# A hybrid attention block in f32: k and v of one half of the second branch by seven products, with the weight sums made in DRAM

## The chip, the core and the metric

The kernel runs on one core of a Trainium2 chip. A core has five engines with queues of their own: TensorE (PE) for matmuls, with its weight load listed apart as PEld, VectorE (DVE), ScalarE (ACT), GpSimd (POOL) and SyncE (SP). Transfers are issued from the queues of SP, ACT and POOL. The metric is the device time of one execution in microseconds, the median over runs. A profiled execution gives a span, from the first to the last recorded instruction, and its own time, which is some 2 us longer.

## The reference

One decoder block over 512 tokens of width 1024. The normalised input is projected, two attention branches of 8 heads of 64 read the projections, each is multiplied by a SiLU gate, projected back, and both are merged by sigmoid gates.

```python
h = rms_norm(x, norm_g[layer])
proj = h @ w_in[layer]
fq, fk, fv, fz, mq, mk, mv, mz, ga, gb, fl = split_cols(proj, IN_SPLITS)
...
y_fox = from_heads(fox_attention(q, k, v, log_f)) * jax.nn.silu(fz)
q = partial_rope(rms_norm(to_heads(mq, MOBA_HEADS), moba_q_g[layer]), positions)
k = partial_rope(rms_norm(to_heads(mk, MOBA_HEADS), moba_k_g[layer]), positions)
v = to_heads(mv, MOBA_HEADS)
y_moba = from_heads(moba_attention(q, k, v)) * jax.nn.silu(mz)
merged = (jax.nn.sigmoid(ga + b_gate[layer, 0]) * (y_fox @ w_fox[layer])
          + jax.nn.sigmoid(gb + b_gate[layer, 1]) * (y_moba @ w_moba[layer]))
x = x + merged @ w_out[layer]
```

The part that the change touches most is `mk` and `mv` for the first four heads of the second branch: 256 columns of k and 256 of v, each the product of the 512x1024 normalised input with a 1024x256 block of `w_in`. The names of blocks are `f` or `m` for the branch, `q`, `k`, `v` or `z`, and `a` or `b` for the half of the heads: `mka` is k of the first half of the second branch.

## The kernel before

Precision: a float32 operand is split into a high part (rounded to the matmul format, by a ScalarE copy) and a low part (the rest, by a VectorE subtraction), and every product is three matmuls, high by high, high by low and low by high. For weights this is `split` (L138, with L141 and L143); the split input is kept in `Gh` and `Gl`, transposed, eight blocks of 128 rows by 512 tokens.

Weights come in as blocks of 512 KB (512 rows by 256 columns) on SP's queue, into the four buffers of the tag "wr". `stream` puts a load and a preparation for each block into two lists, in the order of the list `order` (L997), and `pump` (L189) works the lists off: it issues a load when the buffer four places before has been prepared, and prepares blocks up to three ahead of the unit of matmuls that is about to run.

A unit of an ordinary projection (`unit`, `unit_mm`, L308) is one tile of 128 tokens: 24 matmuls of 256 columns into one PSUM bank (8 row blocks, three matmuls each). For q and k, `evac_qk` copies the bank out (L322), and after every second tile `norm_qk` (L331) computes the norms, with two operations on POOL (L343, L345), and `do_rope` turns the first 16 columns, on POOL too. For v, `evac_v` splits the bank into high and low parts (L352, L353).

The work runs in stages. The start loads and normalises x and computes the first projections. The stage "attention" holds four attention groups, (f,a), (f,b), (m,a) and (m,b), each mixed by `inter` (L1026) with units of projections as filler: `plan` (L1066) says which. With group (f,b) go `mka`, `mva` and `mza`. A group begins with transposes of q and k (`Tr`, `p_qT` and `p_kT`, L528 and L530), copies of them on SP's and ACT's queues (L541, L549 to L551), and memsets on POOL that `zero_kl` (L452) issues once. Within an engine the framework fixes the order of the instructions when the kernel is built; an engine takes them in that order.

The stage "gates" computes the gate projections `ga` and `gb`, for which the kernel uses a scheme of seven products of half the size in place of eight (`group`, L715). The input is cut into four blocks, A11, A12, A21, A22, by halves of the tokens and halves of the rows of x, and the weights likewise. Sums of the input blocks, S1 to S4, are made once by `make_sums` (L265) during the first attention group, stored to DRAM on ACT's queue (L284), and loaded back by `load_sums` (L287) on POOL's queue when "gates" begins. The sums of the weight blocks are made on VectorE (`sub`, L722) in the "wr" buffers. `PRODUCTS` gives the order of the products and the accumulator of each. The last stage, the output projection, uses seven products too, with two sums by accumulating transfers on POOL's queue (L897).

Of the kernel before, what the change touches and what calls it, by code (L numbers as in the profile page):

```python
# [7 lines left out]
F32 = mybir.dt.float32  # L8
F32R = mybir.dt.float32r
AF = mybir.ActivationFunctionType  # L10
OP = mybir.AluOpType
# [18 lines left out]
def fox_moba_kernel(ctx: ExitStack, tc, xT, x, w_in, w_fl, w_fox, w_moba, w_out, cst, rope, out):  # L30
# [171 lines left out]
    def stream(name):  # L202
        first_prep[name] = len(preps)
        if name[0] == "G":
            group(name)
            return
# [54 lines left out]
    S_dram = [dr.tile([4, P, 4, HT], F32, name=f"s_dram{hl}") for hl in "hl"]  # L261
# [3 lines left out]
    def make_sums(k):  # L265
# [6 lines left out]
        for o, x, y, op in ((s3, a[:, 0:HT], a[:, HT:S], OP.subtract), (s1, a[:, HT:S], b[:, HT:S], OP.add),  # L272
                            (s2, s1, a[:, 0:HT], OP.subtract), (s4, b[:, 0:HT], s2, OP.subtract)):
            V.tensor_tensor(out=o, in0=x, in1=y, op=op)
        for i, f in enumerate((f0, f1)):
            hl = [tl("sh", F32R), tl("sl", F32R)]
            A.activation(hl[0], f, AF.Copy)
            V.tensor_tensor(out=hl[1], in0=f, in1=hl[0].bitcast(F32), op=OP.subtract)
            out.extend((d[2 * i:2 * i + 2, :, k, :].rearrange("s p t -> p s t"),
                        t.bitcast(F32).rearrange("p (s t) -> p s t", t=HT)) for d, t in zip(S_dram, hl))  # L280
# [6 lines left out]
    def load_sums():  # L287
        for i in range(4):
            SB.append([stage["pool"].tile([P, 4, HT], F32R, name=f"S{i}{hl}") for hl in "hl"])
            for d, t in zip(S_dram, SB[i]):  # L290
                nc.gpsimd.dma_start(out=t.bitcast(F32), in_=d[i])

    def left(what, k):
        if what[0] == "S":
            return [x[:, k] for x in SB[S_AT[what]]]
        t, kk = int(what[1]) - 1, 4 * (int(what[2]) - 1) + k
        return [x[:, kk, t * HT:(t + 1) * HT] for x in (Gh, Gl)]
# [85 lines left out]
    def first_qk(name, tags):  # L383
# [10 lines left out]
        return banks  # L394

# [316 lines left out]
    PRODUCTS = (("A11", 1), ("S3", 3), ("A12", 2), ("S2", 1), ("S1", 1), ("A22", 3), ("S4", 1))  # L712
    groups = {}

    def group(name):  # L715
# [6 lines left out]
        def sub(o, a, b):  # L722
            V.tensor_tensor(out=o, in0=a, in1=b, op=OP.subtract)

        def load(key, nm, hf):
            def go():
                R[key] = sb.tile([P, 4, CW], F32, name=f"wr_{nm}{hf}", tag="wr", bufs=WR)
                nc.sync.dma_start(out=R[key], in_=w_in[COLS[nm] // CW, :, 4 * hf:4 * hf + 4, :])
            return go

        def prep(n):

            def go():
                if n == 1:
                    sub(R["11"], R["12"], R["11"])
                    sub(R["12"], R["22"], R["12"])
                elif n == 3:
                    sub(R["12"], R["22"], R["11"])
                elif n == 5:
                    sub(R["21"], R["21"], R["12"])  # L740
                key = ("11", "12", "21", "12", "11", "21", "22")[n]
                B[n] = split(R[key], CW, f"{name}{n}")
            return go
        for key, nm, hf, last in (("11", wa, 0, 4), ("12", wb, 0, 5), ("22", wb, 1, 6), ("21", wa, 1, 5)):
# [29 lines left out]
        def evac(n):  # L774
# [8 lines left out]
            elif n == 1:  # L783
                keep(3, 3)
            elif n == 2:
                add(st["u"][0], 0, 1, 2)
# [10 lines left out]
        def finish(q):  # L797
            u, j0 = st["u"][q], 2 * i + 4 * q
            bg = C_BG + (0 if ga else 8)
            for c in range(2):  # L800
                if q == 0:
                    A.activation(u[:, c, :], u[:, c, :], AF.Sigmoid, bias=col(bg + j0 + c))
                else:
                    A.activation(u[:, c, 0:HT], two(st[1])[:, c, :], AF.Sigmoid, bias=col(bg + j0 + c))
                    A.activation(u[:, c, HT:S], u[:, c, HT:S], AF.Sigmoid, bias=col(bg + j0 + c))
# [191 lines left out]
    order = ["fqa", "fka", "fza", "fzb", "fva", "fqb", "fkb", "fvb", "mqa", "mka", "mva", "mza", "mqb", "mkb", "mvb", "mzb", "wf0", "wf1", "wf2", "wf3",  # L997
# [59 lines left out]
    for k, u in enumerate(fz):  # L1057
        u()
        if k < 3:
# [5 lines left out]
    rope_tables()  # L1065
    plan = (("f", "a", C_FQ, C_FK, ["fqb", "fkb", "fvb", "mqa"]),  # L1066
            ("f", "b", C_FQ, C_FK, ["mka", "mva", "mza"]),
# [4 lines left out]
    for n in range(4):  # L1072
# [24 lines left out]
        inter(body + ([following] if n < 3 else []) + tail, fill)  # L1097
# [131 lines left out]
```

## Time and profile before

| What | Value |
|---|---|
| Median of 3 runs | 425.77 us (425.74 to 426.47) |
| The profiled execution's own time | 425.43 us |
| Its span | 423.4 us |
| Matmuls | 2913 recorded |
| Bytes moved by DMA | 58.21 MB, 137 GB/s in the mean |

The page of the profile lists busy time by engine, then the span in 40 slices with the busy share of each in tenths, then the chain of waits followed back from the last instruction, then the costliest groups of instructions (line, engine, operation, output and inputs, count, busy time, mean in ns, idle time before and what ended it), and last the transfers with the time from issue to landing. Views of the trace give the timeline of one engine, the instructions of one line or one tile, and the busy times of all engines in chosen stretches. A row of a timeline has start, duration, engine, line, operation, output and inputs; a row of stretches has begin and end, length, busy time and count for PE, PEld, DVE, ACT and POOL, the granted clock of TensorE as a share, the share of the DMA engines, and GB/s.

### The profile page before, as it was taken

How to read it: one execution, taken by the hardware profiler on the slowest of the kernel's cores; microseconds unless marked ns; L12 is line 12 of the kernel's file. 1: busy time of each engine (PE TensorE's matmuls, PEld its weight loads, DVE VectorE, ACT ScalarE, POOL GpSimd, SP SyncE). 2: the span in 40 equal slices, each digit the busy share in tenths (PEclk: the TensorE clock that was granted, in tenths of full speed). 3: DMA queues.
4: the chain of work that ended last, by engine and by line, in shares of the span. 5: the costliest groups of instructions: out<-in, count | busy, mean ns of one | idle time of the engine just before them, and what ended most of it. 6: DMA issues, size and time to landing. Idle time of an engine off the chain costs nothing.

```text
span 423.4 us, 7713 instructions
## 1 busy us (share of the span) xinstructions
PE 417.7 (99%) x2913; PEld 388.9 (92%) x2913; DVE 326.8 (77%) x570; ACT 269.5 (64%) x515; POOL 106.3 (25%) x120
## 2 busy tenths in 40 slices
PE   8999999999999999999999999999999999999996
PEld 6998899999999998899998888899999989988885
DVE  4679977899967768578676787767979698689883
ACT  4986327778767767567656686756656535686450
POOL 1065730225136550016660202140000000022330
PEclk9999999999999999999999999999999999999999
DMA  7973334666263323314123222473042603696484
GB/s 242 396 257 112 100 101 127 183 198 211 77 209 108 100 78 125 82 45 124 31 96 114 88 74 82 154 279 110 31 170 66 233 2 121 206 253 116 100 142 157
DMA packets 25621, 58.21 MB, mean 137 GB/s; under 512 B 3064, under 2 KB 7856, under 8 KB 25584
## 3 DMA queue, kind: packets, MB, share of 16 engines
q1 hardware_dynamic: 13392, 38.11, 27.7%
q10 hardware_dynamic: 8800, 11.21, 8.7%
q0 software_dynamic: 3392, 8.39, 8.5%
q8 instruction: 23, 0.38, 0.3%
q14 instruction: 14, 0.11, 0.1%
HBM read 48.11 MB, written 6.32 MB: 129 GB/s over the span
## 4 chain that ended last, share of the span: by engine, by line
PE 97%; DMA 1%; SPq 0%; DVE 0%; issue 0%; ACT 0%
PE pb_GB L762 3%; PE pb_GA L762 3%; PE pb_GB L759 3%; PE pb_GA L759 3%; PE pb_GB L761 3%; PE pb_GA L761 3%; PE po L950 3%; PE po L949 3%; PE po L948 3%; PE lg L565 2%; PE pv L620 2%; PE pv L619 2%; PE lg L564 2%; PE pf L690 2%; PE pf L689 2%; PE pm L690 2%
## 5 line engine op out<-in xcount | busy, mean ns | idle before, releaser
L343 POOL TENSOR_TENSOR ff<-ss,mh 128x8 f32<-128x8 f32 x16 | 32.0, 2005 | 71.0 <-DVE ss L341 63.2
L567 DVE CUSTOM_DVE_ANT_0 p<-lg,mask 128x128 f32<-128x128 f32 (+1 forms) x64 | 30.6, 488 | 15.7 <-PE lg L565 15.3
L569 ACT ACTIVATE p<-p,negm 128x128 f32<-128x128 f32 (+1 forms) x64 | 35.6, 557 | 10.0 <-DVE negm L567 9.7
L897 POOL DMA_DIRECT2D wr_o<-in_w_out_dram x4 | 4.9, 1293 | 95.4 <-DMA wr_o<-in_w_out_dram 87.2
L143 DVE TENSOR_TENSOR wl_GA<-wr_ga,wh_GA 128x1024 fp32r<-128x1024 f32 x14 | 16.9, 1223 | 7.6 <-ACT wh_GA L141 5.8
L141 ACT ACTIVATE wh_GA<-wr_ga 128x1024 fp32r<-128x1024 f32 x14 | 14.6, 1059 | 9.9 <-PE pb_GA L761 4.9
L141 ACT ACTIVATE wh_GB<-wr_gb 128x1024 fp32r<-128x1024 f32 x14 | 14.6, 1059 | 9.5 <-PE pm L689 3.5
L564 PE MATMUL lg<-KH,QS 128*128 128x128 f32 (+1 forms) x64 | 20.3, 327 | 0.0
L910 ACT ACTIVATE wh_o<-wr_o 128x1024 fp32r<-128x1024 f32 x14 | 14.8, 1060 | 8.2 <-PE pb_GB L761 2.8
L911 DVE TENSOR_TENSOR wl_o<-wr_o,wh_o 128x1024 fp32r<-128x1024 f32 x14 | 17.0, 1221 | 3.8 <-ACT wh_o L910 3.8
L143 DVE TENSOR_TENSOR wl_GB<-wr_gb,wh_GB 128x1024 fp32r<-128x1024 f32 x14 | 16.9, 1222 | 3.5 <-ACT wh_GB L141 3.5
L645 DVE TENSOR_TENSOR ypair<-pv,ysh 64x512 f32<-64x512 f32 x16 | 11.0, 687 | 5.8 <-ACT ysh L644 5.5
L337 DVE TENSOR_REDUCE ss<-sq 128x8 f32<-128x512 f32 x16 | 10.9, 679 | 4.6 <-ACT sq L336 4.5
L538 DVE SCALAR_TENSOR_TENSOR QS<-p_qT,cs,QS 64x512 fp32r<-64x512 f32 x16 | 12.0, 750 | 2.4 <-ACT QS L537 2.0
L759 PE MATMUL pb_GA<-Gh,wh_GA 128*128 128x256 f32 x48 | 13.6, 282 | 0.0
L761 PE MATMUL pb_GA<-Gl,wh_GA 128*128 128x256 f32 x48 | 13.5, 281 | 0.0
L762 PE MATMUL pb_GA<-Gh,wl_GA 128*128 128x256 f32 x48 | 13.5, 281 | 0.0
L762 PE MATMUL pb_GB<-Gh,wl_GB 128*128 128x256 f32 x48 | 13.5, 281 | 0.0
L761 PE MATMUL pb_GB<-Gl,wh_GB 128*128 128x256 f32 x48 | 13.4, 281 | 0.0
L759 PE MATMUL pb_GB<-Gh,wh_GB 128*128 128x256 f32 x48 | 13.3, 281 | 0.0
L542 DVE SCALAR_TENSOR_TENSOR KL<-p_kT,cs,KH 64x512 fp32r<-64x512 f32 x16 | 12.0, 749 | 1.3 <-ACT KH L540 0.8
L537 ACT ACTIVATE QS<-p_qT,cs 64x512 fp32r<-64x512 f32 x16 | 10.9, 680 | 3.3 <-DVE QS L538 2.2
(459 smaller groups left out, 1792.8 us busy)
## 6 DMA issues: line engine op xcount, KB each, us to landing
wr_ga<-in_w_in_dram SPq DMA_DIRECT2D x8, 512.0 KB
wr_gb<-in_w_in_dram SPq DMA_DIRECT2D x8, 512.0 KB, 5.1
wr_o<-in_w_out_dram SPq DMA_DIRECT2D x8, 512.0 KB, 12.6
xt<-in_xT_dram SPq DMA_DIRECT2D x8, 256.0 KB, 6.9
x<-in_x_dram SPq DMA_DIRECT2D x8, 256.0 KB, 6.0
KH<-KH ACTq DMA_DIRECT2D x16, 128.0 KB, 4.8
s_dramh<-sum_sh ACTq DMA_DIRECT2D x8, 256.0 KB, 5.5
s_draml<-sum_sl ACTq DMA_DIRECT2D x8, 256.0 KB, 2.5
```

Source lines behind the costliest of these rows:

```text
L141: A.activation(hi[:, :, 0:n], src, AF.Copy)
L143: eng.tensor_tensor(out=lo[:, q, 0:n], in0=src[:, q], in1=hi[:, q, 0:n].bitcast(F32), op=OP.subtract)
L343: G.tensor_tensor(out=f2, in0=ss.rearrange("p t h -> p (t h)"), in1=mh, op=OP.pow)
L564: T.matmul(lg[:, :n], qs[:, qt], kh[:, :n], start=True, stop=False)
L567: V.tensor_tensor_reduce(pt, lg[:, :n], mask[:, 512 - n:512], -0.125, 3.0e38, op0=OP.add, op1=OP.min, accum_out=mkn[:, hh, i:i + 1])
L569: A.activation(pt, pt, AF.Exp, bias=mkn[:, hh, i:i + 1], scale=-1.0, accum_out=rs[:, hh, i:i + 1])
L690: T.matmul(p, lo[:, k, cc], yh, start=False, stop=(k == 3))
L759: T.matmul(o, hi[:, k, cc], lh, start=(n < 3 and c == 0 and k == 0), stop=False, skip_group_check=True)
L761: T.matmul(o, hi[:, k, cc], ll, start=False, stop=False, skip_group_check=True)
L762: T.matmul(o, lo[:, k, cc], lh, start=False, stop=(k == 3), skip_group_check=True)
L910: A.activation(wide(hi), wide(R[key, c]), AF.Copy)
L911: V.tensor_tensor(out=wide(lo), in0=wide(R[key, c]), in1=wide(hi).bitcast(F32), op=OP.subtract)
```

## The change

`mka` and `mva` together are the product of a 512x1024 input with a 1024x512 weight. They are now computed as `GKa`, seven products of 256x512 by 512x256: `group_kv`. Four products need sums of the input, which are the S1 to S4 of the gates, loaded from DRAM in sixteen transfers on SP's queue (`rows`); four need sums of the weight blocks (T1 to T4), which `weight_sums` makes in DRAM: four copies and four accumulating transfers on POOL's queue, placed behind the last POOL instruction of `rope_tables`. SP then loads seven blocks instead of four. Products of one accumulator follow each other, and partial results are copied out (`keep`) and added (`k_half`, `v_half`).

The signs of the sums S1, S2 and S4 are turned in `make_sums`. Their DRAM tile holds high and low parts side by side, so that the gates load them in four transfers instead of eight. In the gate groups A12 now comes second, one weight sum is made by an accumulating transfer on POOL's queue into the "wr" buffer, the VectorE operations for weight sums go from four to three, and the sigmoid takes its input with scale -1. In the second attention group the first part of the next group's work (`following`) moves behind the first step of the tail.

```diff
@@ def stream(name)
-            group(name)
+            (group_kv if name[1] == "K" else group)(name)
@@ def make_sums(k), load_sums
-    S_dram = [dr.tile([4, P, 4, HT], F32, name=f"s_dram{hl}") for hl in "hl"]
+    S_dram = dr.tile([4, P, 4, 2, HT], F32, name="s_dram")
...
-        for o, x, y, op in ((s3, a[:, 0:HT], a[:, HT:S], OP.subtract), (s1, a[:, HT:S], b[:, HT:S], OP.add),
-                            (s2, s1, a[:, 0:HT], OP.subtract), (s4, b[:, 0:HT], s2, OP.subtract)):
-            V.tensor_tensor(out=o, in0=x, in1=y, op=op)
+        V.tensor_tensor(out=s3, in0=a[:, 0:HT], in1=a[:, HT:S], op=OP.subtract)
+        V.tensor_tensor(out=s1, in0=b[:, HT:S], in1=a[:, HT:S], op=OP.subtract)
+        V.scalar_tensor_tensor(s2, s1, -1.0, a[:, 0:HT], op0=OP.mult, op1=OP.subtract)
+        V.scalar_tensor_tensor(s4, s2, -1.0, b[:, 0:HT], op0=OP.mult, op1=OP.subtract)
...
-            SB.append([stage["pool"].tile([P, 4, HT], F32R, name=f"S{i}{hl}") for hl in "hl"])
-            for d, t in zip(S_dram, SB[i]):
-                nc.gpsimd.dma_start(out=t.bitcast(F32), in_=d[i])
+            SB.append(stage["pool"].tile([P, 4, 2, HT], F32R, name=f"S{i}"))
+            nc.gpsimd.dma_start(out=SB[i].bitcast(F32), in_=S_dram[i])
@@ new, behind unit_z
+    KV_PRODUCTS = (("A11", "11", 1), ("A12", "21", 2), ("S2", "T2", 1), ("S3", "T3", 3), ("S1", "T1", 1), ("S4", "22", 1), ("A22", "T4", 3))
+    WT = {}
+
+    def weight_sums(name):
+        half = name[2]
+        blk = {f"{i + 1}{j + 1}": w_in[COLS[f"m{c}{half}"] // CW, :, 4 * i:4 * i + 4, :]
+               for i in range(2) for j, c in enumerate("kv")}
+        tt = {t: dr.tile([P, 5, CW], F32, name=f"t{t}_{name}")[:, 0:4] for t in ("T3", "T1", "T2", "T4")}
+        for t, a in (("T3", "12"), ("T1", "11"), ("T2", "11"), ("T4", "21")):
+            G.dma_start(out=tt[t], in_=blk[a])
+        for t, a in (("T3", blk["22"]), ("T1", blk["12"]), ("T2", tt["T3"]), ("T4", tt["T2"])):
+            G.dma_start(out=tt[t], in_=a, accum_op=OP.add)
+        WT[name] = {**blk, **tt}
+
+    def group_kv(name):
...
+            def load():
+                raw[0] = sb.tile([P, 4, CW], F32, name=f"wr_{name}{n}", tag="wr", bufs=WR)
+                nc.sync.dma_start(out=raw[0], in_=WT[name][KV_PRODUCTS[n][1]])
...
+        def rows(what):
+            if what[0] == "S":
+                for k in range(4):
+                    f = t2("y", 15, f"{what}{k}", dt=F32R)
+                    nc.sync.dma_start(out=f.bitcast(F32).rearrange("p (q t) -> p q t", q=2), in_=S_dram[S_AT[what], :, k])
+                    st[what, k] = [f[:, 0:HT], f[:, HT:S]]
+
+        def product(n):
+            what, _, b = KV_PRODUCTS[n]
+            new = b not in st
+            if new:
+                st[b] = (tp if b == 2 else pj)(f"pj{b}_{name}")
+            hi, lo = B[n]
+            for t in range(2):
+                o = st[b][:, t * CW:(t + 1) * CW]
+                tt = slice(t * P, (t + 1) * P)
+                for k in range(4):
+                    lh, ll = (x[:, tt] for x in (st[what, k] if what[0] == "S" else left(what, k)))
+                    T.matmul(o, lh, hi[:, k, :CW], start=(new and t == 0 and k == 0), stop=False,
+                             skip_group_check=True)
+                    T.matmul(o, lh, lo[:, k, :CW], start=False, stop=False, skip_group_check=True)
+                    T.matmul(o, ll, hi[:, k, :CW], start=False, stop=(k == 3), skip_group_check=True)
+
+        def keep(n, b):
+            st["e", n] = t2("y", 15, f"e{n}_{name}") if n == 2 else t2("u", 4, f"e{n}_{name}")
+            A.activation(st["e", n], st[b], AF.Copy)
+
+        def k_half(h, n, b):
...
+            V.tensor_tensor(out=QN[kn][:, ts, :].rearrange("p t c -> p (t c)"), in0=st[b], in1=st["e", n], op=OP.add)
+            norm_qk(kn, ts)
+            do_rope(kn, ts)
+
+        def v_half(h):
...
+            f = st[1]
+            if h:
+                f = st["e", 4]
+                V.tensor_tensor(out=f, in0=st[3], in1=f, op=OP.add)
+            for t in range(2):
+                v = VT[vn][:, 2 * h + t]
+                pv = f[:, t * CW:(t + 1) * CW].rearrange("p (h d) -> p h d", d=HD)
+                A.activation(v[:, :, 0:HD], pv, AF.Copy, scale=-1.0)
+                V.scalar_tensor_tensor(v[:, :, HD:P], pv, -1.0, v[:, :, 0:HD].bitcast(F32), op0=OP.mult, op1=OP.subtract)
+
+        def unit(n):
+            def go():
+                for what in {0: ("S2", "S3"), 3: ("S1",), 4: ("S4",)}.get(n, ()):
+                    rows(what)
+                product(n)
...
@@ group(name)
-    PRODUCTS = (("A11", 1), ("S3", 3), ("A12", 2), ("S2", 1), ("S1", 1), ("A22", 3), ("S4", 1))
+    PRODUCTS = (("A11", 1), ("A12", 2), ("S3", 3), ("S2", 1), ("S1", 1), ("A22", 3), ("S4", 1))
...
+                if key == "12":
+                    G.dma_start(out=R[key], in_=rows(wb, 1), accum_op=OP.add)
...
-                if n == 1:
-                    sub(R["11"], R["12"], R["11"])
-                    sub(R["12"], R["22"], R["12"])
-                elif n == 3:
-                    sub(R["12"], R["22"], R["11"])
-                elif n == 5:
-                    sub(R["21"], R["21"], R["12"])
+                if n == 3:
+                    plus(R["11"], R["11"], R["12"])
+                elif n == 4:
+                    plus(R["21"], R["21"], R["11"])
+                    plus(R["11"], R["11"], R["22"], OP.subtract)
@@ the stages
+    with behind(mybir.EngineType.Pool):
+        weight_sums("GKa")
     plan = (("f", "a", C_FQ, C_FK, ["fqb", "fkb", "fvb", "mqa"]),
-            ("f", "b", C_FQ, C_FK, ["mka", "mva", "mza"]),
+            ("f", "b", C_FQ, C_FK, ["GKa", "mza"]),
...
-        inter(body + ([following] if n < 3 else []) + tail, fill)
+        inter(body + (tail[:1] + [following] + tail[1:] if n == 1 else [following] + tail if n < 3 else tail), fill)
```

59 lines of the change are left out of this document (46 added, 13 removed).

## The prediction

> **What bounds the kernel now.** I read the page from the top: span, busy shares, the 40 slices, then the chain that ended last.
>
> ```profile
> span 423.4 us, 7713 instructions
> PE 417.7 (99%) x2913; PEld 388.9 (92%) x2913; DVE 326.8 (77%) x570; ACT 269.5 (64%) x515; POOL 106.3 (25%) x120
> ...
> PE   8999999999999999999999999999999999999996
> ...
> DVE  4679977899967768578676787767979698689883
> ACT  4986327778767767567656686756656535686450
> ...
> PEclk9999999999999999999999999999999999999999
> ...
> PE 97%; DMA 1%; SPq 0%; DVE 0%; issue 0%; ACT 0%
> ```
>
> TensorE sets the end: it is busy 99% of the span, its slices show a dent only in the first and the last, its clock row is full everywhere, and 97% of the chain is its own work. So a matmul taken away shortens the run by one issue interval, as long as the other engines keep up. VectorE is next with 77%. The sum below is made against the profiled execution's 425.43 us (span 423.4 and 2.03 around it); the median of the three runs, 425.77, lies 0.34 above it, and I add that at the end.
>
> What a matmul costs is the distance between starts, not the 0.28 us of a row, since they overlap. From the timeline of TensorE, and from a stretch with only 256-column matmuls (columns: stretch, length, busy time and count of PE, PEld, DVE, ACT, POOL, clock, DMA share, GB/s):
>
> ```profile
> 128.40 0.28 PE L315 MATMUL pj_mka<-wh_mka,Gh 128*128 128x256 f32 x1
> 128.52 0.28 PE L316 MATMUL pj_mka<-wl_mka,Gh 128*128 128x256 f32 x1
> 128.64 0.29 PE L317 MATMUL pj_mka<-wh_mka,Gl 128*128 128x256 f32 x1
> ```
>
> ```profile
> 285.00:295.00 10.00, 10.00 (x87) 10.00 (x86) 7.77 (x9) 5.23 (x7) 0.00 (x0) 1.00 0.39 130
> ```
>
> The rows stand 0.12 us apart; 10.00 us over 87 matmuls is 0.115.
>
> **Removed from TensorE.** k and v of this half were 8 units of 24 matmuls, 192:
>
> ```profile
> L315 PE MATMUL pj_mka<-wh_mka,Gh x32: 278/280/367, 128.4 to 142.6; 128*128 128x256 f32 x32
> ...
> L322 ACT ACTIVATE qn_mka<-pj_mka x4: 383/384/384, 132.5 to 144.2; 128x256 f32<-128x256 f32 x4
> ```
>
> ```profile
> L315 PE MATMUL pj_mva<-wh_mva,Gh x32: 277/280/367, 143.3 to 161.3; 128*128 128x256 f32 x32
> ```
>
> Each name has 32 matmuls on L315, and as many on L316 and L317. The seven products have 2 row tiles x 4 blocks x 3 matmuls = 24 each, 168. So 24 fall away, all others keep number and size: between 24 x 0.115 = 2.76 and 24 x 0.12 = 2.88; I take **-2.8 us**. Nothing else in the change takes work off TensorE.
>
> **Added beside it, in the same window.** The stretch from 126 to 162 us holds these 192 matmuls. Here it is with two dense stretches:
>
> ```profile
> 30.00:60.00 30.00, 30.00 (x164) 25.80 (x163) 28.94 (x60) 14.60 (x26) 18.57 (x19) 1.00 0.40 123
> 80.00:110.00 30.00, 30.00 (x244) 29.40 (x244) 27.73 (x65) 24.51 (x59) 10.25 (x7) 1.00 0.58 173
> 126.00:162.00 36.00, 36.00 (x290) 35.30 (x290) 25.90 (x59) 25.77 (x58) 19.91 (x28) 1.00 0.29 89
> ```
>
> ```profile
> L143 DVE TENSOR_TENSOR wl_GA<-wr_ga,wh_GA 128x1024 fp32r<-128x1024 f32 x14 | 16.9, 1223 | 7.6 <-ACT wh_GA L141 5.8
> L141 ACT ACTIVATE wh_GA<-wr_ga 128x1024 fp32r<-128x1024 f32 x14 | 14.6, 1059 | 9.9 <-PE pb_GA L761 4.9
> ...
> L645 DVE TENSOR_TENSOR ypair<-pv,ysh 64x512 f32<-64x512 f32 x16 | 11.0, 687 | 5.8 <-ACT ysh L644 5.5
> ...
> L537 ACT ACTIVATE QS<-p_qT,cs 64x512 fp32r<-64x512 f32 x16 | 10.9, 680 | 3.3 <-DVE QS L538 2.2
> ```
>
> Seven weight blocks are split instead of four: 3 x 1.223 on VectorE and 3 x 1.059 on ScalarE. VectorE also gets three additions of 512 columns (two for k, one for v), at the 0.687 of the nearest row: 3.67 + 2.06 = +5.7 us. ScalarE gets three copies of a product out of PSUM at 0.68 and loses the four of L322 at 0.384: 3.18 + 2.04 - 1.54 = +3.7 us. The splits of v keep number and shape.
>
> TensorE's time for the window falls to 36.0 - 2.8 = 33.2 us, in which VectorE has 25.9 + 5.7 = 31.6 (95%) and ScalarE 25.8 + 3.7 = 29.5 (89%). How much of this can be used without a stall is not shown for this mix, so I bound it. From 30 to 60 us VectorE ran 28.94 of 30 (96.5%) with TensorE full: stall 0. At the 27.73 of 30 (92.4%) of the stretch from 80 to 110 it needs 31.6 / 0.924 = 34.2, a stall of 1.0. For ScalarE the densest of the three, 24.51 of 30 (81.7%), would need 29.5 / 0.817 = 36.1, a stall of 2.9, but neither row shows an engine that stalls, so they are no limits. I take **+1.0**, since the stretch from 80 to 110 is also attention with projections between, and keep 0 and 2.9 for the range.
>
> **Sums of x for the products.** Sixteen loads of 256 KB stand newly on SP's queue. Those of S2 and S3 go out at the first unit and have two units until use. Those of S1 wait for buffers that matmuls of S2 read, and in the built order they are used 47 matmuls later; S4's buffers come from S3, 87 matmuls later. By 0.115 that is 5.4 and 10.0 us, less where wide attention matmuls are missing, so about 5. The nearest landing times of 256 KB:
>
> ```profile
> x<-in_x_dram SPq DMA_DIRECT2D x8, 256.0 KB, 6.0
> ...
> s_draml<-sum_sl ACTq DMA_DIRECT2D x8, 256.0 KB, 2.5
> ```
>
> So a wait between 0 and 6.0 plus some queueing less 5.4, about 2; the row of 2.5 is the same array's: I take **+0.4**. Behind S1's waiting loads on SP stand the weight blocks of mqb and the KL and Q copies of the next group; its first logits come 6.2 us after its transposes in the built order, now 7.7, and that is part of the same bound.
>
> **Weight sums in DRAM.** Eight transfers go on POOL's queue behind the rope tables: four copies, then four accumulating ones, of which T2's waits for T3's and T4's for T2's. Behind each wait stands POOL work for the first attention group.
>
> ```profile
> 35.61 0.77 POOL L366 TENSOR_TENSOR tab_mk<-rp,cs 128x32 f32<-128x32 f32 x1
> 36.34 1.04 POOL L345 TENSOR_TENSOR qn_fqa<-qn_fqa,ff 128x512 f32<-128x512 f32 x1
> 44.93 5.71 POOL L343 TENSOR_TENSOR ff<-ss,mh 128x8 f32<-128x8 f32 x2 [7.55 <-DVE ss L339]
> 50.61 2.58 POOL L345 TENSOR_TENSOR qn_fka<-qn_fka,ff 128x512 f32<-128x512 f32 x2
> 53.26 0.99 POOL L452 MEMSET KL<- 64x512 f32 x2
> ...
> 55.71 0.52 POOL L452 MEMSET Q<- 64x512 f32 x1
> 76.84 1.64 POOL L343 TENSOR_TENSOR ff<-ss,mh 128x8 f32<-128x8 f32 x1 [20.62 <-DVE ss L341]
> ```
>
> ```profile
> 65.62 0.60 PE L530 MATMUL p_kT<-ident,qn_fka 128*128 128x128 f32 x4
> ```
>
> ```profile
> L897 POOL DMA_DIRECT2D wr_o<-in_w_out_dram x4: 1194/1244/1491, 370.8 to 382.4; - x4
> ...
> DMA to landing us min/median/max: 6.7/7.9/9.9
> ```
>
> ```profile
> 261.17 0.78 POOL L291 DMA_DIRECT2D S0h<-s_dramh  x1
> ...
> 270.54 0.54 POOL L291 DMA_DIRECT2D S1h<-s_dramh  x1 [8.04 <-PE p_b L609]
> ...
> DMA to landing us min/median/max: 3.8/5.0/6.6
> ```
>
> An accumulating transfer of 512 KB took 1.24 us to issue and 7.9 to land (L897, into SBUF; one between two places in DRAM isn't in this trace). By the built order: copies from 36.34 by 0.78 each to 39.5, the second qn_fqa to 40.5, T3's accumulate at about 41.3 (its copy must land), landed at 49.2; T2's to 57.1, with the 5.71 of L343 between them; T4's issue to 58.3, the two of L345 to 60.9, the memsets to 63.9. p_kT reads qn_fka at 65.62, 4.7 us after 60.9. So **0**: the matmuls of fva and before cover it. The cover is gone when the two landings in a row take over 7.9 x 2 + 4.7 = 20.5 us together.
>
> **The gate groups.** Each loses one subtraction of 1.22 on VectorE, in stretches where TensorE has no gap to give back, so 0. The sums are loaded in four transfers instead of eight, and the block made by an accumulating transfer stands ahead of them on POOL.
>
> ```profile
> 276.65 0.36 PE L759 MATMUL pb_GA<-Gh,wh_GA 128*128 128x256 f32 x1
> ...
> 280.86 0.28 PE L759 MATMUL pb_GA<-S0h,wh_GA 128*128 128x256 f32 x1
> ```
>
> A 1 MB tile needs the room that S0h and S1h had, so S0 goes out at about 270.5 + 1.2 = 271.7 instead of 261.2. It is now used in the third product instead of the second: 280.86 - 2.8 + 24 x 0.115 = 280.8. That leaves 9.1 us for a load of 1 MB; its 512 KB halves landed in 3.8 to 6.6 each (the line below the S0h rows), which I double to 7.6 to 13.2, the low end being that of quiet moments. I take 0, since the median of the halves doubled, 10.0, is within 0.9 of the room, and keep 0 to 4.1. Signs (L272, the sigmoid's scale) cost nothing: same number of instructions.
>
> **Sum.** -2.8 + 1.0 + 0.4 = -1.4: profiled 424.0, median 425.77 - 1.4 = **424.4 us**.
>
> **The rivals.**
> (a) All of the 24 matmuls is kept: no stall at 95%, as from 30 to 60 us, and the loads of S1 land like s_draml. 425.77 - 2.8 = 423.0. Against it: each split block now feeds 24 matmuls, where it fed 48, so a late split is felt sooner.
> (b) VectorE or ScalarE becomes the bound of the window and takes it all back: at the 81.7% of ScalarE the stall is 2.9, so 425.77 - 2.8 + 2.9 = 425.9. For it: both run denser here than over any other attention stretch. Against it: neither shows a stall at those shares.
> (c) Slower: POOL's chain of accumulating transfers ends after 65.62, and qn_fka is late for p_kT. TensorE runs its instructions in order, so everything behind waits. It decides once two landings together exceed 20.5 us. At 12 each the chain is 41.3 + 24 + 1.2 + 2.6 = 69.1, 3.5 late: 425.77 - 1.4 + 3.5 = 427.9. For it: these transfers read and write DRAM while x and weights still arrive, and POOL is slow in this stretch, as L343 shows with 5.71 / 2 = 2.86 us here and 1.64 later. Against it: DMA is only 40% busy from 30 to 60 us.
>
> On (c) the Trainium skill, "SBUF — State Buffer", section "Who interferes with whom", says that a VectorE instruction with two SBUF inputs holds off a GpSimd instruction that reads SBUF, and that a DMA issued by GpSimd can be starved of the port its descriptors need. The slower L343 beside a VectorE at 96.5% agrees with its first half; no run here shows the second. By its example of 3.1 us in place of 0.62, an estimate, eight issues would cost POOL some 20 us more and (c) would be the outcome.
> (d) Slower, in the gates: S0 lands 2 to 4 us late, or the GA block's accumulate holds POOL longer; with the rest as forecast 424.4 + 3 = 427.4.
>
> **How the numbers follow.** A measurement of this kernel tells about 0.2% from no change, 0.85 us: faster is below 424.9, slower above 426.6. Forecast 0.39 (own range 423.3 to 424.9), (a) 0.15, (b) 0.20, (c) 0.16, (d) 0.10. Faster is the forecast and (a): 0.54. Same is most of (b) and a little of (d): 0.20. Slower is the rest: 0.26. The range goes from 422.7, just below (a), to 427.9, the price of (c), and leaves out the longer landings of (c).
>
> **What would show it.** Right: the page of the changed kernel has some 24 matmuls fewer, TensorE's slices stay at 9, the rows of p_kT stand at about 65.6, and the start of the third attention group comes 1 to 2 us earlier than before with VectorE above 90% in the window. Wrong: idle time of TensorE put down to qn_fka near 66 us (c), to S1's or S2's rows (loads), to wl of this group or to VectorE additions (b), or to S0 near 281 us (d).

## The result, and the profile after

The changed kernel takes 433.38 us (median of 4 runs, 432.53 to 433.67) against 425.88 us of the kernel before in the same comparison: a ratio of 1.0175, with an interval of 1.016 to 1.0189. It is 7.5 us slower; 424.4 was forecast, with a range up to 427.9. The profiled execution has a span of 431.4 us, 8.0 more than before.

From the page of the changed kernel: span, busy shares, slices, chain.

```profile
span 431.4 us, 7728 instructions
PE 418.6 (97%) x2889; PEld 387.6 (90%) x2889; DVE 329.0 (76%) x572; ACT 271.3 (63%) x517; POOL 114.5 (27%) x128
...
PE   8999999999999599999999999999999999999996
...
PEclk9999999999999989999999999999999999999999
...
PE 59%; DMA 4%; POOL 1%; ACT 1%; issue 1%; DVE 1%; ACTq 0%; DVEq 0%; POOLq 0%
```

The 24 matmuls are gone (2889 after 2913), yet TensorE's row has a hole in the fourteenth slice and its clock a dent in the fifteenth. The view of what TensorE waited for names the hole (columns: total, times, longest):

```profile
PE lg L671 <- DMA KH<-KH: 4.8, 1, 4.8
...
PE pj_mqa L315 <- ACT qn_mqa L322: 0.8, 1, 0.8
...
PE p_kT L637 <- POOL qn_mkb L381: 0.6, 1, 0.6
```

KH is the high part of a head's k, which ACT's queue copies to the other 64 partitions. The wait belongs to the third head of the second group, in the middle of GKa. The chain of waits, cut to this place, shows what made it late:

```profile
139.60 0.10 DVE negm L674
...
139.72 0.71 ACT p L676 x2
140.43 0.95 ACT wh_GKa L141
141.38 0.25 ACT QS L644
...
141.85 0.61 ACT yhf L779
142.47 0.06 ACT KH L647
...
143.08 6.87 DMA KH<-KH
...
150.08 0.30 PE lg L671
```

ScalarE takes its instructions in order. Ahead of KH stand an exponential that waits for a maximum on VectorE, and a split of a GKa block. Here is the same place before, on ScalarE and then on TensorE:

```profile
139.84 0.68 ACT L537 ACTIVATE QS<-p_qT,cs 64x512 fp32r<-64x512 f32 x1
140.43 0.67 ACT L540 ACTIVATE KH<-p_kT,cs 64x512 fp32r<-64x512 f32 x1
...
141.13 0.56 ACTq L541 DMA_DIRECT2D KH<-KH  x1
```

```profile
139.64 0.60 PE L530 MATMUL p_kT<-ident,qn_fkb 128*128 128x128 f32 x4
...
146.64 0.22 PE L564 MATMUL lg<-KH,QS 128*128 128x128 f32 x1
```

And the transposes after:

```profile
138.59 0.60 PE L637 MATMUL p_kT<-ident,qn_fkb 128*128 128x128 f32 x4
```

Before, the copy went out 1.5 us after the transposes began, and the logits started 5.5 us after that. The page gives 4.8 us for such a copy, but that is the landing of a single one, issued at 119.73. A transfer counts up a semaphore, a counter that others can wait for, as it lands; by the records of this counter in the trace, the copy issued at 141.13 had landed at 143.45, after 2.3 us. The DMA engines agree: from 143.0 on they were all but empty (kernel before, columns as in the prediction).

```profile
141.60:143.00 1.40, 1.40 (x14) 1.40 (x13) 1.03 (x2) 1.24 (x2) 1.32 (x4) 1.00 0.86 186
143.00:143.40 0.40, 0.40 (x6) 0.40 (x5) 0.21 (x1) 0.40 (x1) 0.32 (x2) 1.00 0.03 5
```

So some 3.1 us were spare: 146.64 - 143.45 = 3.2, less 0.1 between a landing and the first matmul. Now the copy goes out 4.5 us after the transposes (+3.0), takes 6.87 (+4.6), and TensorE arrives 0.5 earlier. Less the 3.1, that is 5.0, against a recorded wait of 4.8. By the same sum, an estimate, the late issue alone would have cost 0.4 us and the slow copy alone 2.0: it took both.

Behind the wait TensorE ran at half its clock (stretches of the changed kernel, columns as in the prediction):

```profile
145.00:150.00 5.00, 0.29 (x3) 0.08 (x1) 2.75 (x6) 3.86 (x5) 3.87 (x4) 1.00 0.85 245
150.00:152.00 2.00, 1.92 (x11) 1.95 (x12) 1.43 (x6) 0.24 (x1) 1.84 (x5) 0.64 1.08 283
152.00:154.00 2.00, 2.00 (x9) 1.90 (x9) 1.94 (x3) 1.33 (x5) 0.07 (x1) 0.51 1.05 345
154.00:156.00 2.00, 2.00 (x18) 1.96 (x17) 1.50 (x4) 0.39 (x1) 0.00 (x0) 1.00 1.08 342
```

At 0.64 and 0.51 for 2 us each, 2 x 0.36 + 2 x 0.49 = 1.7 us are lost on top. The DMA share of 1.05 to 1.08 in the same rows is the other finding: the sums of x for the next products and the blocks of mqb are all under way.

A second place is earlier. SP starts to load S2 and S3 while ACT still stores the last sums; the KH copy of the second head, behind those stores on ACT's queue, is held. SP's queue, then ACT's:

```profile
116.34 12.02 SPq L439 DMA_DIRECT2D S<-s_dram  x8
```

```profile
119.34 0.37 ACTq L285 DMA_DIRECT2D s_dram<-sum_sl  x1
124.11 0.47 ACTq L648 DMA_DIRECT2D KH<-KH  x1
124.63 0.38 ACT L322 ACTIVATE qn_mqa<-pj_mqa 128x256 f32<-128x256 f32 x1 [5.53 <-DMA s_dram<-sum_sl]
```

The last row names a store, but the landing that ended this stand is another one. The trace records the semaphore of every transfer: the issue at 124.11 waits for the one on which the copy of Q counts that ACT issued at 116.22, and its last count comes at 124.04. The stores issued at 117.44 and 119.34 landed only at 126.1 and 126.8. So ACT's whole queue stands 4.4 us for an older copy of its own. Before, the same KH copy went out at 119.73 without a stand: it used the semaphore of a weight block that SP had issued at 113.48 and that had landed at 117.9. SP's new loads at 116.34 and 117.81 take the semaphores that came next, and so KH's issue gets the one of Q. TensorE felt 0.8 us of this stand, the row of pj_mqa above.

### The profile page after: what moved, and what is told of

Read it like the earlier page. It is cut to its first block, busy times and chain, and to the rows that moved or that the text cites. A ratio compares the mean times of both kernels' runs of the same rounds, so it can differ in the third digit from the quotient of the medians.

```text
span 431.4 us, 7728 instructions
## 1 busy us (share of the span) xinstructions
PE 418.6 (97%) x2889; PEld 387.6 (90%) x2889; DVE 329.0 (76%) x572; ACT 271.3 (63%) x517; POOL 114.5 (27%) x128
## 3 DMA queue, kind: packets, MB, share of 16 engines
q0 software_dynamic: 4544, 14.68, 15.8%
## 4 chain that ended last, share of the span: by engine, by line
PE 59%; DMA 4%; POOL 1%; ACT 1%; issue 1%; DVE 1%; ACTq 0%; DVEq 0%; POOLq 0%
PE pb_GB L871 3%; PE pb_GB L874 3%; PE pb_GB L873 3%; PE po L1062 3%; PE po L1061 3%; PE po L1060 3%; PE pb_GA L871 2%; PE pb_GA L874 2%; PE pb_GA L873 2%; PE pf L795 2%; PE pf L796 2%; PE pm L796 2%; PE pf L797 2%; PE pm L797 2%; PE pm L795 2%; DMA KH<-KH 2%
## 5 line engine op out<-in xcount | busy, mean ns | idle before, releaser
L671 PE MATMUL lg<-KH,QS 128*128 128x128 f32 (+1 forms) x64 | 20.5, 328 | 5.0 <-DMA KH<-KH 4.8
L871 PE MATMUL pb_GA<-S,wh_GA 128*128 128x256 f32 x64 | 18.2, 284 | 0.0
L874 PE MATMUL pb_GB<-S,wl_GB 128*128 128x256 f32 x64 | 18.0, 281 | 0.0
L871 PE MATMUL pb_GB<-S,wh_GB 128*128 128x256 f32 x64 | 18.0, 281 | 0.0
L874 PE MATMUL pb_GA<-S,wl_GA 128*128 128x256 f32 x64 | 18.0, 281 | 0.0
L873 PE MATMUL pb_GB<-S,wh_GB 128*128 128x256 f32 x64 | 18.0, 281 | 0.0
L873 PE MATMUL pb_GA<-S,wh_GA 128*128 128x256 f32 x64 | 17.9, 280 | 0.0
L671 PEld LDWEIGHTS lg<-KH,QS 128*128 128x128 f32 x64 | 12.2, 191 | 6.0 <-issue 5.1
L723 DVE TENSOR_TENSOR ptl<-p_b,pth 128x512 fp32r<-128x512 f32 x16 | 10.9, 684 | 8.4 <-ACT pth L722 8.3
L751 ACT ACTIVATE ysh<-pv 64x512 f32<-64x512 f32 x16 | 9.5, 593 | 9.1 <-PE pv L727 3.4
```

The costliest lines, as they stand in the source:

```text
L671: T.matmul(lg[:, :n], qs[:, qt], kh[:, :n], start=True, stop=False)
L871: T.matmul(o, hi[:, k, cc], lh, start=(n < 3 and c == 0 and k == 0), stop=False, skip_group_check=True)
L873: T.matmul(o, hi[:, k, cc], ll, start=False, stop=False, skip_group_check=True)
L874: T.matmul(o, lo[:, k, cc], lh, start=False, stop=(k == 3), skip_group_check=True)
```

## The experiments

Theory A: the transfers of the sums crowd the DMA engines (stores held, KH slowed). B: the extra work of VectorE and ScalarE. C: the accumulating transfers on POOL. D: the gates. The waits in the table are those of the one profiled execution of each run; it lies some 2 to 3 us above the median in e1 (430.87) and e7 (428.66), and as much below it in e2 (431.65), e11 (430.46) and e16 (433.15).

| Run | Median, us | Ratio to before (interval) | Longest waits of TensorE from 110 to 180 us |
|---|---|---|---|
| changed kernel | 433.38 | 1.016 to 1.0189 | KH 4.8 |
| e1 no loads of sums | 428.74 | 1.0057 to 1.012 | KH 2.6 |
| e2 last block first | 434.22 | 1.0141 to 1.0264 | S 5.2, KH 0.9 |
| e3 gates alone | 427.31 | 1.0024 to 1.0056 | none |
| e4 weight sums alone | 425.45 | 0.9987 to 1.0012 | none |
| e5 small splits | 429.66 | 1.0076 to 1.0121 | S 0.8, KH 0.5 |
| e6 both, e1 and e5 | 428.45 | 1.004 to 1.0076 | VectorE's KL 1.3 |
| e7 gates, sum on VectorE | 426.70 | 1.0006 to 1.0039 | 0.4 |
| e8 logits later | 434.99 | 1.0199 to 1.0236 | S 2.5, keep 1.4, QS 1.3 |
| e9 GKa, gates of before | 431.32 | 1.0109 to 1.0183 | KH 4.7 |
| e10 KH ahead of QS | 438.42 | 1.0287 to 1.032 | Q 4.4, S 3.0 |
| e11 mqb in the second group | 433.18 | 1.015 to 1.0233 | split of mza 2.0 |
| e12 mza first | 436.73 | 1.0239 to 1.0284 | S 3.7, rinv 2.4 |
| e13 24 matmuls back | 431.00 | 1.0116 to 1.015 | KH 1.0 |
| e14 splits half on POOL | 437.63 | 1.0265 to 1.0299 | S 4.3, qn_mqa 2.9 |
| e15 all relieved | 426.15 | 1.0002 to 1.0029 | VectorE's KL 0.7 |
| e16 sums on POOL's queue | 436.23 | 1.0198 to 1.0269 | S 6.3 |

**e1**, the loads of the sums left out.

```diff
-                for what in {0: ("S2", "S3"), 3: ("S1",), 4: ("S4",)}.get(n, ()):
-                    rows(what)
-                    lh, ll = (x[:, tt] for x in (st[what, k] if what[0] == "S" else left(what, k)))
+                    lh, ll = (x[:, tt] for x in (left("A11" if what[0] == "S" else what, k)))
```

> The sixteen loads of sums of x are left out: the four products that need S1 to S4 read the unsummed first block of the input in their place, with the same number of matmuls. Theory A (the loads crowd the DMA engines twice: at 116 to 124 us they slow the stores of the sums, behind which ACT's queue is held 4.8 us, and at 143 us they slow the KH copy for which TensorE waits 4.8 us): both waits are gone, TensorE has no wait over 1 us between 110 and 180 us, and the time is 433.4 - 4.8 (KH) - 2.3 (slow matmuls behind that wait) - 0.9 (mqa) = 425.4 us or up to 1.5 less. Rival B (VectorE and ScalarE are too full in this stretch, whatever the transfers do): still 430 or more, with TensorE waiting for VectorE or ScalarE. Rival C (the accumulating transfers on POOL): still 431 or more.

Measured 428.74: between A and B. The five times fall into two lots, 428.5 to 428.7 and 430.9 to 431.1; the trace is of the second. ACT's hold near 119 us is gone, as A says (no gap over 0.8 us there), so the loads cause it; KH's issue uses the semaphore of a weight block of SP again, as in the kernel before. But KH is still waited for:

```profile
PE lg L669 <- DMA KH<-KH: 2.6, 1, 2.6
```

Its copy still goes out 4.0 us after the transposes (144.51 after 140.48), and by the semaphore's records it takes 5.4 us although no sums are loaded: SP has issued two blocks of mqb from 140.47 on. So the hold near 119 us isn't what makes KH late; the order on ScalarE is, with a copy that other transfers slow. The loads cost 4.6 us of the 7.5 by the medians and 3.7 by the ratios (1.0175 less 1.0088), not all.

**e2**, the S2 loads in another order.

```diff
-                for k in range(4):
+                for k in (3, 0, 1, 2) if what == "S2" else range(4):
```

> Only the order of the S2 loads changes: the block that is stored last is loaded first, so that SP's queue waits for all stores before it loads anything. Theory A: the stores are no longer slowed, ACT's queue is held under 1.5 us near 119 us instead of 4.8, ScalarE reaches the KH copy near 140 instead of 142.4 us, TensorE's wait for KH falls from 4.8 to 0 to 2 us, and the time is 426 to 429.5. Rival A2 (only the crowding at 143 us counts): the wait for KH stays at 3 us or more and the time at 431 or more. Rival B: 431 or more with KH no longer waited for.

The KH copy near 119 us is issued without a stand (ACT's largest gap there is 1.4 us) and the wait for KH fell to 0.9, as A expected, and nothing was won: 434.22 (431.65 to 438.0). TensorE now waits 5.2 us for sums that land late. The expected time was wrong because the loads have no slack either.

**e3** and **e4**, parts of the change alone.

```diff
-            ("f", "b", C_FQ, C_FK, ["GKa", "mza"]),
+            ("f", "b", C_FQ, C_FK, ["mka", "mva", "mza"]),
```

> The change without GKa: mka and mva are units of 24 matmuls as before, no weight sums in DRAM, no loads of S in the attention stage, the interleaving as before; what stays is the new signs and layout of the sums, the four 1 MB loads and the new order and accumulating transfer in the gate groups. Theory A: 425.9 plus or minus 0.6. Rival D (the gates lose several us by the late load of S0): 427.5 or more, with a wait of TensorE behind 275 us.

```diff
+        for t, a in (("T3", "12"), ("T1", "11"), ("T2", "11"), ("T4", "21")):
+            G.dma_start(out=tt[t], in_=blk[a])
+        for t, a in (("T3", blk["22"]), ("T1", blk["12"]), ("T2", tt["T3"]), ("T4", tt["T2"])):
+            G.dma_start(out=tt[t], in_=a, accum_op=OP.add)
```

> The kernel before with the eight transfers of the weight sums added on POOL's queue, their results not used. Theory A: p_kT of the first group starts within 0.8 us of before (65.6 us), the time is 425.9 to 426.7. Rival C (the chain of accumulating transfers makes qn_fka late): 428 or more.

e4 takes exactly as long as before: C is out. e3 is 1.9 us slower, between what A and D expected; D's place (S0) is wrong, since nothing waits behind 275 us for S0. A part of the loss stands beside the accumulating transfer of a weight block. POOL's queue, then VectorE, in e3:

```profile
333.76 0.89 POOL L842 DMA_DIRECT2D wr_gb<-in_w_in_dram  x1 [27.58 <-DVE wl_wm L143]
```

```profile
342.07 1.23 DVE L832 TENSOR_TENSOR wr_gb<-wr_gb,wr_gb 128x1024 f32<-128x1024 f32 x1 [1.89 <-DMA wr_gb<-in_w_in_dram]
```

The block is loaded, then added to by the transfer issued at 333.76, and is there at 342.07, 8.3 us later; VectorE stands 1.9 us for it. Matmul by matmul against the kernel before, TensorE is 0.5 us late when the gates begin, 1.1 at 316 and 2.1 at 350; some 1 us of this arises between 340 and 348, beside this wait. That the wait makes it is argued, not shown: e7 below leaves it open.

**e5** and **e6**, three quarters of three weight splits left out, with and without the loads.

```diff
-                B[n] = split(raw[0], CW, f"{name}{n}")
+                A.activation(hi[:, 0:1, 0:CW], raw[0][:, 0:1], AF.Copy)
+                V.tensor_tensor(out=lo[:, 0:1, 0:CW], in0=raw[0][:, 0:1], in1=hi[:, 0:1, 0:CW].bitcast(F32), op=OP.subtract)
```

> Three of the seven weight blocks of GKa (products 3 to 5, counted from 0) are split only in their first quarter, which stands for the other three; this leaves out 2.4 us of ScalarE and 2.8 us of VectorE, all loads stay. Theory A (crowded DMA engines decide): KH is still waited for, 2 us or more, and the time stays at 430 or more. Theory B (the extra work of VectorE and ScalarE ahead of the KH copy decides): the copy is issued near 140.5 instead of 143.1 us, the wait falls below 1.5 us and the time to 428 or less. If both count alike, 428.5 to 430.5.

> Both left out: the sixteen loads of sums (the unsummed first block of the input in their place) and three quarters of three weight splits. If the two together are the whole loss between 110 and 180 us, TensorE waits for nothing over 0.7 us there, its clock stays full, and the time is 425.5 - 2.8 + 0.2 to 1.9 of the gates (the run with the gates alone lay 1.9 above before) = 422.9 to 424.6. If something else of GKa costs time, 426 or more.

e5: the copy goes out 2.2 us after its transposes instead of 4.5, KH is waited for 0.5 us, the clock stays full, and 3.7 us are won by the medians. So B is as real as A. e6 shows that the two don't add up: 428.45, 0.3 under e1 by the medians and 1.3 by the ratios (1.0088 less 1.0058). What is left are small waits in a row, none of them large (e6):

```profile
PE p_ri L702 <- DVE KL L655: 1.3, 1, 1.3
...
PE p_b L722 <- DVE ptl L729: 0.3, 1, 0.3
PE p_a L722 <- DVE ptl L729: 0.3, 1, 0.3
PE p_a L722 <- ACT rinv_t L704: 0.3, 1, 0.3
```

**e7**, e3 with its weight sum on VectorE.

```diff
-                if key == "12":
-                    G.dma_start(out=R[key], in_=rows(wb, 1), accum_op=OP.add)
+                if n == 2:
+                    plus(R["12"], R["12"], R["22"])
```

> The run with the gates alone, but the weight sum of its accumulating transfer is made on VectorE again (four operations per group instead of three). If the accumulating transfer costs the gates their time (block landed, then added, before its split): 425.3 to 426.3. If the order of products or the 1 MB loads do: 427 or more, as before this edit.

426.70 (425.18 to 428.66) lies between the two answers, and its interval overlaps that of e3: inconclusive on how much of the gates' loss is the transfer and how much the order of products.

**e8**, the third head's logits behind the second head's work.

```diff
+            if n == 0:
+                body[5], body[6] = body[6], body[5]
...
+                    with (behind(mybir.EngineType.PE) if i == 0 and br + half == "fb" and h == 2 else ExitStack()):
+                        T.matmul(lg[:, :n], qs[:, qt], kh[:, :n], start=True, stop=False)
```

> The changed kernel with the logits of the third head of the second group placed behind the work of the second head: 31 more matmuls, some 3.7 us, between the transposes and the first use of KH; nothing is left out. The wait for KH falls from 4.8 to 1.2 us or less. If that wait and the slow clock behind it were the loss, the time is 433.4 - 3.7 - 1.7 = 428.0, plus or minus 1.5. If the lateness only moves to the next use (S1's loads, or VectorE), 431 or more with a wait for S or wh_GKa.

KH isn't waited for any more, and the kernel is no faster: TensorE comes sooner to the products of S1, whose loads aren't there, and then to GKa's keep. The lateness moved.

**e9**, GKa with the gates of before (the diff of the gates undone).

> GKa with the gates of before: the order of products, the four VectorE sums, the eight loads and the unsigned sums of x of the kernel before. GKa then reads sums that aren't its own, so its k and v are not the reference's; the work is the same. If the attention stage holds the loss: 431.5 to 433.5, with the wait for KH and the slow clock behind it as in the changed kernel, and the lag behind the kernel before the same at the first gate product as at the end (within 0.5 us). If the gates have a share as in the run with the gates alone: 430 to 431.5.

431.32: the wait for KH is 4.7 again. By the medians the parts add up with e3: 433.4 - 431.3 = 2.1 for the gates here, 1.9 there. But the interval of e9 overlaps that of the changed kernel, so the 2.1 is not clear of noise. GKa with the gates of before costs 5.8 us; the later place of `following` is part of this and was not run apart.

**e10**, KH ahead of QS.

```diff
+                    A.activation(kh[me, :], pk[me, :], AF.Copy, scale=gk[me, :])
+                    nc.scalar.dma_start(out=kh[ot, :].bitcast(F32), in_=kh[me, :].bitcast(F32))
                     A.activation(qs[me, :], pq[me, :], AF.Copy, scale=gq[me, :])
```

> The changed kernel with the copy of KH and its transfer written ahead of QS in every group's transposes (nothing left out). If ScalarE's order ahead of the KH copy decides (maximum, exponential, weight split, QS, then KH): the transfer goes out 0.7 us or more sooner after its transposes, the wait for KH falls to 3.5 us or less, and the time to 429.5 to 432.5. If QS or VectorE then becomes late instead: 432.5 or more.

Worse by 5: TensorE now waits 4.4 us for a copy of Q, until 124.6 us, and 3.0 us for sums. Putting KH ahead makes QS and Q late instead, as the second expectation said.

**e11** and **e12**, other work beside GKa.

```diff
-            ("f", "b", C_FQ, C_FK, ["GKa", "mza"]),
-            ("m", "a", C_MQ, C_MK, ["mqb", "mkb", "mvb"]),
+            ("f", "b", C_FQ, C_FK, ["GKa", "mza", "mqb"]),
+            ("m", "a", C_MQ, C_MK, ["mkb", "mvb", "mzb"]),
```

> mqb moves from the third attention group into the second, mzb from the fourth into the third: 96 more matmuls (11 us) stand beside the same attention work of the second group, with two more weight splits. Theory (the second group has too little TensorE work beside its chain of transposes, logits, maxima and copies): no wait over 1.5 us between 110 and 190 us, no slow clock, 425 to 428.5. If only the fourth group is now short instead: the same up to 190 us, and 3 us or more lost between 200 and 280 us, 428.5 or more. If the extra work of VectorE decides wherever GKa stands: 430 or more with waits as before.

```diff
-            ("f", "b", C_FQ, C_FK, ["GKa", "mza"]),
+            ("f", "b", C_FQ, C_FK, ["mza", "GKa"]),
```

> mza, which has 96 matmuls of 512 columns in two units and two weight splits, stands ahead of GKa in the second group. The loads of the sums then have 11 us more until use, and the first half of the group has less VectorE work. If crowding and fullness ahead of the KH copy decide: no wait for KH over 1 us, 425 to 428.5. If the end of GKa is then late for the third group's transposes: a wait of TensorE for qn_mka or its rope on POOL of 3 us or more, 430 or more.

e11: KH is waited for 0.2 us only, but a split of mza 2.0 and sums 0.4: 433.18 (430.46 to 435.08), nothing won. e12 reads k and v of the third group ahead of GKa's last units; it waits for S, for the rinv copy and for a split, 436.73.

**e13**, 24 matmuls put back: the fourth product is computed twice, and its sum counts double.

```diff
                 product(n)
+                if n == 3:
+                    product(n)
```

> The changed kernel with the 24 matmuls of product 3 done twice (its sum is then counted double, so k and v are not the reference's): TensorE has as many matmuls as before, 24 more of them between the transposes and the logits that wait for KH. If the chain holds this stage and not TensorE, the added 2.8 us fill the wait: KH is waited for 2 us or less, and the time is 431 to 433.5, not longer than the changed kernel's 433.4. If TensorE's work counts in full there: 435.5 or more.

431.00, 2.4 us less than the changed kernel, with 24 matmuls more. The wait shrinks and the clock stays full (e13, waits, then a stretch):

```profile
PE lg L673 <- DMA KH<-KH: 1.0, 1, 1.0
```

```profile
150.00:152.00 2.00, 1.49 (x12) 1.16 (x10) 1.67 (x4) 1.40 (x6) 1.92 (x4) 1.00 1.05 249
152.00:154.00 2.00, 2.00 (x15) 2.00 (x16) 0.00 (x0) 0.00 (x0) 0.32 (x1) 1.00 1.05 288
```

The parts add up to about that: 2.8 us of work more, 3.8 of the wait and 1.7 of the slow clock less, is 2.7 less. So at this place the matmuls taken away were worth less than nothing: they covered the chain, and the slow clock made the gap cost more than its length.

**e14**, the low parts of the splits half on POOL.

```diff
-                B[n] = split(raw[0], CW, f"{name}{n}")
+                B[n] = split(raw[0], CW, f"{name}{n}", True)
```

> The low parts of the seven weight blocks of GKa are made half on VectorE and half on POOL (nothing left out). VectorE's fullness alone: it gains 0.6 us per block, 4 us in all, the wait for KH falls to 2.5 us or less and the time to 428.5 to 431. If POOL and VectorE hold each other up, as the one subtraction of 2.18 us beside a POOL multiplication suggests (1.22 alone): 433 or more, with VectorE's splits longer than half of 1.22 us.

437.63. The view of groups for this stretch shows why, VectorE's half first, then POOL's:

```profile
L143 DVE TENSOR_TENSOR wl_GKa<-wr_GKa,wh_GKa 128x512 fp32r<-128x512 f32 x7 | 8.0, 1140 | 1.1 <-ACT wh_GKa L141 1.1
```

```profile
L143 POOL TENSOR_TENSOR wl_GKa<-wr_GKa,wh_GKa 128x512 fp32r<-128x512 f32 x7 | 10.0, 1424 | 5.9 <-ACT wh_GKa L141 5.8
```

Half the elements take VectorE 1.14 us where all of them took 1.22.

**e15**, e9 with the edits of e6.

> GKa with the gates of before, without the sixteen loads of sums (the unsummed first block of the input in their place) and with three quarters of three weight splits left out. If the parts add up: 428.45 (the run with both left out) minus 2.0 (gates) = 426.4, plus or minus 0.7, still not the 422.7 that 24 matmuls less would give. If the three causes are the whole of the loss: 422.7 to 424.

426.15, as the sum of the parts said, and still 1.0002 to 1.0029 times the time before. The 422.7 for 24 matmuls fewer isn't reached even with the three causes taken away or cut down; its first product of GB starts at 313.30 us, 0.7 after that of the kernel before, where 2.8 ahead were due.

**e16**, the sums loaded on POOL's queue.

```diff
-                    nc.sync.dma_start(out=f.bitcast(F32).rearrange("p (q t) -> p q t", q=2), in_=S_dram[S_AT[what], :, k])
+                    nc.gpsimd.dma_start(out=f.bitcast(F32).rearrange("p (q t) -> p q t", q=2), in_=S_dram[S_AT[what], :, k])
```

> The sixteen loads of sums go out on POOL's queue instead of SP's (nothing left out). If the semaphores that ACT's KH issue shares with SP's loads, and SP's queue, are what holds: ACT is held under 2 us near 119 us, 429 to 431.5. If the DMA engines themselves are crowded, whichever queue issues: 432 or more, with KH or S waited for 3 us or more; POOL's own chain (norms of mqa) late by the issue times is a further loss.

ACT isn't held near 119 us any more (no gap over 0.9), and KH's issue uses the semaphore of SP's weight block, so the hold does come from the loads on SP, by way of the semaphores. KH is waited for 0.2 us only, but the products of S1 start only at 150.26, after a wait of 6.3 us for the sums: 436.23.

No version with GKa was faster than the kernel before.

## Why the prediction was wrong, point by point

- **What bounds the kernel.** TensorE at 99% with a chain of 97% was read rightly, and the conclusion, that a matmul less is an interval less, failed. A busy TensorE was itself the cover: its order spaces transposes and logits so that copies, maxima and splits fit in between. At the KH copy 3.1 us were spare, more than the 2.8 taken away, and the page's 4.8 us for the copy would have made it 0.7; what outgrew it was the later issue (3.0) and the slower copy (4.6) together. e13 shows that the 2.8 us are not a gain there.
- **-2.8 us.** The count is right (2889 after 2913), the value is not.
- **+1.0 us for VectorE and ScalarE.** This is one of the two steps that failed. I compared busy shares over 36 us with shares that stretches had borne. The shares were not what filled up: in the same stretch of the changed kernel VectorE was busy 28.7 and ScalarE 27.4 of 36 us. What decided was the order in one queue over 4 us: exponential, split, QS, yhf, KH. e5 prices the splits at 3.7 us of the total, with a VectorE that is 76% busy in the span, no fuller than before.
- **+0.4 us for the sums.** This is the other. I asked how late S1 itself would be, by the row of 2.5 us where the other half of the same array had 5.5, and said that the KL and Q copies behind it on SP belong to that bound. I did not ask what 4 MB more in 35 us do to other queues: the semaphore that held ACT for 4.4 us, and the KH copy at 6.87 us instead of 2.3. e1 prices the loads at 4.6 us (3.7 by the ratios).
- **The clock** was not in the sum: a wait of 4.8 us cost 1.7 more behind it.
- **0 for the accumulating chain** held, though narrowly: TensorE has no wait for qn_fka, and e4 costs nothing. POOL's queue in the changed kernel:

```profile
41.09 0.87 POOL L412 DMA_DIRECT2D tT_GKa<-in_w_in_dram  x1 [0.87 <-DMA tT_GKa<-in_w_in_dram]
...
52.09 0.81 POOL L412 DMA_DIRECT2D tT_GKa<-tT_GKa  x1 [8.12 <-DMA tT_GKa<-in_w_in_dram]
...
60.75 0.87 POOL L412 DMA_DIRECT2D tT_GKa<-tT_GKa  x1 [3.54 <-DMA tT_GKa<-tT_GKa]
61.36 2.34 POOL L345 TENSOR_TENSOR qn_fka<-qn_fka,ff 128x512 f32<-128x512 f32 x2
```

  The two landings took 19.7 us together (41.09 to 60.75), where 15.8 were forecast and 20.5 were the limit; p_kT stands at 66.41.
- **0 for the gates** was wrong by some 2 us (1.9 in e3). I asked for S0 (rival d), which was in time; in e3 the block behind load and accumulating transfer was late.
- **The rivals.** (b) came nearest in its mechanism, but took back only the gain: 425.9. (c) and (d) were slower than before, each by one wait at another place; neither wait is there. None had a copy that is issued late and slowed as well, and KH is not among the rows named as signs of being wrong.

What stays open: how the loss of e6 and e15 divides over the small waits (VectorE's KL, the copies of p_a and p_b), what the later place of `following` does to it, and how the gates' 2 us divide between transfer and order.

## What to carry to other kernels

Before work is taken from the engine that bounds a kernel, find, for each operand that arrives without a wait, how long before its use it lands: this one operand's landing, not the median of its kind (here 2.3 us, not 4.8). Three things are paid out of this spare time together: the work removed from the engine, what every added instruction puts ahead of the operand on an in-order queue, and what added transfers do to its own transfer. Where their sum is larger (here 0.5 + 3.0 + 4.6 against 3.1), the gain is not there, however full the engine. So price an added transfer at what it does to the transfers and queues beside it, small copies first, not at its own lateness.

## What had not been expected of the hardware

- **The clock after a wait.** It fell to 0.5 for 3.4 us with waits of 4.8 us (changed kernel), 3.7 (e12), 2.5 to 2.6 (e1, e8) and once 1.8 (e12, at 183.5 us), and stayed at 1.00 behind 2.4 (e12, at 176.1), 2.0 (e11), 1.3 (e6) and 1.0 (e13); so the length of the wait alone doesn't decide. The Trainium skill, "TensorE: Matmul & The Clock Gate", section "Why this matters for your kernels", advises no gaps over about 3 us, since one idle window brings the clock to half; the half clock agrees, and here 2.5 us, and once 1.8, were already enough.
- **VectorE and POOL.** One split on VectorE took 2.18 us instead of 1.22 beside a multiplication on POOL (VectorE, then POOL, changed kernel):

```profile
135.47 2.18 DVE L143 TENSOR_TENSOR wl_GKa<-wr_GKa,wh_GKa 128x1024 fp32r<-128x1024 f32 x1
```

```profile
135.27 1.29 POOL L777 TENSOR_TENSOR rinv_bc<-zs_fza,rinv_bc 128x512 f32<-128x512 f32 x1
```

  From POOL's end at 136.56 to VectorE's at 137.65 are 1.1 us, about one split alone. With e14 it agrees with the Trainium skill, "SBUF — State Buffer", section "Who interferes with whom": a VectorE instruction with two SBUF inputs and a GpSimd instruction that reads SBUF exclude each other.
- **A shared semaphore held a whole queue.** ACT stood 4.4 us for the landing of its own copy of Q, because the next KH copy counted on the same semaphore; SP's added loads had only shifted which transfer gets which. In all kernels of this document whose KH issue there shares the semaphore of that copy of Q (the changed kernel, e5, e8, e9, e10, e11, e13) ACT stood 3.8 to 4.7 us. Where it has that of a weight block that SP issued near 114 us (the kernel before, e1 to e4, e6, e7, e12, e15, e16), it stood under 0.3, and in e14, with a block issued at 116.7, 1.2 us.
